# Two mixture-of-experts stages and an S5 scan: a float32 gather, an earlier overflow check, a ring of 18 tiles, S5 products by turns

## The chip, the cores and the metric

The kernel runs on one core of a Trainium2 chip. A core has TensorE (PE, with its weight loads shown as PEld), VectorE (DVE), ScalarE (ACT), GpSimd (POOL) and SyncE (SP, here the queue that issues nearly all DMA). The metric is the device time of one execution in microseconds (us), the median of several runs.

## The reference

256 tokens of width 1024 pass through a first block of two layers (an even mixer, a mixture of experts, an odd mixer, a mixture of experts) and then a second block. The change touches the experts (both layers) and the S5 half of the odd mixer:

```python
def hier_moe(h, ...):                       # 32 experts, 4 groups of 8
    g_top = argmax(hf @ w_group + b_group)  # one group per token
    e_logits = (hf @ w_expert + b_expert)[rows, g_top]
    top_p, top_j = top_k(softmax(e_logits), 2)
    gates = g_w * top_p / sum(top_p)
    # each chosen expert, 1024 -> 512 -> 1024:
    hidden = silu(xb @ w_gate[e]) * (xb @ w_up[e])
    out[token] += (hidden @ w_down[e]) * gate

def s5_mixer(u, ...):                       # 32 groups of 16 channels, 64 complex states each
    bu = einsum('gpc,btgc->btgp', b_bar, u)
    states = associative_scan(x_t = lam_bar * x_{t-1} + bu_t)
    y = einsum('gcp,btgp->btgc', c_mat, states).real + d_skip * u
    z = gelu(y); return z * sigmoid(z @ w_glu)
```

All inputs and outputs are float32. The second block (retention, SSD and a SwiGLU, two layers) is untouched.

## The kernel before

**Stages.** The program is one straight run of instructions for each engine, with four stages in front of the second block: the even mixer, MoE 0, the odd mixer, MoE 1. `moe` handles the experts in eight groups of four; each expert has 32 slots (`SLOTS`), so that a group's four experts fill 128 rows. `expert_group` does, for each group: a *gather* (line 731), products of the token matrix with a one-hot matrix `oh` that picks each slot's token; the gate and up products (line 738), the four experts on TensorE's four column groups of 32, expert after expert in the innermost loop; the down products (line 775); and the scatter back to tokens (lines 785 and 786).

**Weights.** A group needs 24 tiles of 1 MB (8 gate, 8 up, 8 down). `expert_weights` issues them on SP (line 689) into a ring of SBUF tiles: `ring(n, 3, 3)` takes n tiles of the pool `u8` (13 tiles in all) and three each of two other pools. `RINGS = (10, 4)` are the two values of n: the first for MoE 1 and for the first two groups of MoE 0, the second for the later groups of MoE 0, in which pieces of the odd mixer's preparation (`middle`) run as well. A tile's next load waits until TensorE has read it. `AHEAD = 3` rounds of the first group's loads are issued before the stage begins.

**Tokens.** The router's normalised tokens are split for the gather into a high and a low part in TensorE's reduced format (`h_hi`, `h_lo`, 128 x 1024 for each of two token halves): ACT writes the high parts (lines 532 and 535), POOL one low part (line 534), DVE the other in two halves (`low`, line 539). Between them DVE runs the router's chain of small operations (lines 543 to 589), which ends in the slot positions `pos` and in `oh` (line 719). `keep_warm` (line 239) issues products whose results nobody reads.

**Check.** If an expert has more than 32 tokens, `overflowing` computes the rest: every engine loads the largest count (`values_load`, line 663) and branches (`tc.If`, line 664). It stands ahead of group 2, behind five `keep_warm` products. In these data no expert overflows, and the branch jumps over the code.

**S5.** `s5_steps` is a generator; a table (`OPLAN`) says between which steps of the attention its eight parts run. For each n of 8, `turn(n)` makes the input products (line 1675) and DVE and POOL rotate them (lines 1680 to 1683); `scan(n)` runs the recurrence on DVE (line 1693) and rotates back (DVE line 1694, POOL line 1695); `project(n)` multiplies with C (lines 1706, 1711, 1713) into the 32 columns of n. Its 18 products (each float32 product shows as two records) all go to one column group. TensorE's order in the same stretch also holds the projections of the attention, line 317 (`whl` is a weight split by ACT line 293 and DVE line 298).

Of the kernel before, what the change touches and what calls it, by code (L numbers as in the profile page):

```python
# [147 lines left out]
class Model:  # L148
# [369 lines left out]
    def moe(self, l, ahead=None, middle=None, after=None):  # L518
# [114 lines left out]

        n_groups = 32 // GROUP
        for g in range(n_groups):
            last = g == n_groups - 1
            if g == 2:
                self.keep_warm(WARM["check"])
                self.overflowing(l, over["n"], h_hi, h_lo, over["gates"])
# [8 lines left out]
            self.rest = self.expert_group(g, weights, h_hi, h_lo, pos, gate, () if g else (lambda: low(4), gates, beyond), last)  # L648
# [12 lines left out]
    def overflowing(self, l, cint, h_hi, h_lo, gov):  # L661
        nc, tc = self.nc, self.tc
        n = nc.values_load(cint[0:1, 0:1], min_val=0, max_val=T)
        with tc.If(n > SLOTS):
            hT = self.blocks(NK)
            for j0 in range(0, NK, 2):
                pt = self.psum("mm")
                for j in (j0, j0 + 1):
                    for t in range(2):
                        o = (j - j0) * T + t * P  # L670
                        for i, hh in enumerate((h_hi, h_lo)):
                            nc.tensor.matmul(pt[:, o:o + P], hh[t][:, j, :].bitcast(F32), self.ident, start=j == j0 and t == 0 and i == 0,
                                             stop=j > j0 and t == 1 and i == 1, skip_group_check=True)
# [34 lines left out]
    def expert_group(self, g, weights, h_hi, h_lo, pos, gate, meanwhile, last):  # L708
        nc = self.nc
        loads, wg, wu, wd = weights  # L710
        for _ in loads:
            pass
# [9 lines left out]
        for f in meanwhile[:1]:  # L722
            f()
# [1685 lines left out]
```

## Time and profile before

| | |
|---|---|
| median of three runs | 2721.52 us (2717.72 to 2726.39) |
| profiled execution | 2722.02 us, span 2720.2 us |
| TensorE busy | 2421.8 us, 89% of the span |
| VectorE busy | 1261.8 us, 46% |
| granted TensorE clock, mean | 0.957 of full |
| DMA | 660.97 MB, mean 243 GB/s |

How to read it: the profiled execution is one run on the chip; its span is the time from the first to the last recorded instruction, 1.8 us less than the device time. "Busy" shares are means over stages with different limits: the stages lie at about 0 to 186 us (even mixer), to 690 (MoE 0), to 860 (odd mixer), to 1330 (MoE 1), and the second block fills the rest.

### The profile page before, as it was taken

What the parts mean: (1) busy time and instruction counts of PE and PEld (TensorE: products, weight loads), DVE (VectorE), ACT (ScalarE), POOL (GpSimd) and SP (SyncE); (2) the same over time, 40 slices, a digit from 0 to 9 for tenths busy, and PEclk for the clock granted to TensorE, in tenths of its full rate; (3) what the DMA queues carried; (4) which work ended last, traced back from release to release, by engine and by line L of the source; (5) the groups of instructions that cost most, each with busy time, mean ns of one, the idle gap of its engine ahead of it and who ended that gap; (6) DMA issues with size and microseconds to landing.
All of it is one profiled execution on the core that took longest, in us unless ns stands there. A gap on an engine that the chain in (4) does not pass through costs nothing.

```text
span 2720.2 us, 40356 instructions
## 1 busy us (share of the span) xinstructions
PE 2421.8 (89%) x16793; PEld 1811.6 (67%) x16793; DVE 1261.8 (46%) x2071; ACT 950.9 (35%) x1567; POOL 498.9 (18%) x428
## 2 busy tenths in 40 slices
PE   8997777777988778777799998999999999899998
PEld 7862232222776222222489988999988999899997
DVE  5751122201654001000466677565655667855664
ACT  6431100001354000000345565544444455554443
POOL 1120000100321000000223065221113315531110
PEclk9998878899999899989999999999999999999999
DMA  5368999999328999999754533455555353345553
GB/s 184 108 233 356 352 371 411 421 421 407 114 74 315 422 395 421 421 421 421 272 170 140 183 128 109 157 185 173 186 186 170 125 180 130 125 140 185 172 194 139
DMA packets 208793, 660.97 MB, mean 243 GB/s; under 512 B 26554, under 2 KB 33116, under 8 KB 161500
## 3 DMA queue, kind: packets, MB, share of 16 engines
q1 hardware_dynamic: 202148, 657.23, 63.6%
q8 instruction: 135, 2.21, 0.3%
q10 hardware_dynamic: 6456, 1.08, 0.2%
q14 instruction: 54, 0.44, 0.0%
HBM read 657.22 MB, written 1.05 MB: 242 GB/s over the span
## 4 chain that ended last, share of the span: by engine, by line
PE 42%; DMA 13%; DVE 4%; POOL 3%; ACT 2%; issue 1%; SPq 0%; POOLq 0%; ACTq 0%; DVEq 0%
PE ps_mm L317 38%; DMA wx<-in_moe_w_down_dram 5%; DMA wx<-in_moe_w_gate_dram 4%; DMA wx<-in_moe_w_up_dram 4%; DVE whl L298 2%; ACT whl L293 1%; DVE latri L2005 1%; PE ps_sml L2055 1%; PE ps_sml L2019 1%; DVE cv L1871 1%; POOL xn L1956 1%; PE ps_sml L1935 1%; DVE yf L2094 0%; POOL yf L1907 0%; POOL whl L298 0%
## 5 line engine op out<-in xcount | busy, mean ns | idle before, releaser
L317 PE MATMUL ps_mm<-u,whl 128*128 128x256 f32 x8448 | 1056.7, 286 | 25.6 <-POOL whl L298 15.4
L317 PEld LDWEIGHTS ps_mm<-u,whl 128*128 128x128 f32 x8448 | 1035.1, 194 | 37.5 <-POOL whl L298 17.4
L298 DVE TENSOR_TENSOR whl<-w,whl 128x1024 fp32r<-128x1024 f32 x432 | 558.5, 1296 | 437.5 <-ACT whl L293 436.5
L293 ACT ACTIVATE whl<-w 128x1024 fp32r<-128x1024 f32 x472 | 497.3, 1058 | 537.7 <-PE ps_mm L317 509.7
L738 PE MATMUL ps_mm<-wx,xe 128*32 128x512 f32 x2048 | 375.1, 704 | 135.6 <-DMA wx<-in_moe_w_up_dram 92.8
L738 PEld LDWEIGHTS ps_mm<-wx,xe 128*32 128x32 f32 x2048 | 81.4, 125 | 400.5 <-DMA wx<-in_moe_w_up_dram 166.9
L317 PE MATMUL ps_mm<-whl,u 128*128 128x512 f32 x1440 | 343.2, 395 | 3.6 <-ACT u L305 1.8
L317 PEld LDWEIGHTS ps_mm<-whl,u 128*128 128x128 f32 x1440 | 267.3, 189 | 63.6 <-ACT u L305 2.8
L775 PE MATMUL ps_mm<-wx,hid 128*32 128x512 f32 x1024 | 216.0, 613 | 46.2 <-DMA wx<-in_moe_w_down_dram 35.0
L759 DVE TENSOR_TENSOR sl<-sl,ps_mm 128x512 f32<-128x512 f32 x16 | 11.0, 688 | 410.5 <-PE ps_mm L738 301.2
L775 PEld LDWEIGHTS ps_mm<-wx,hid 128*32 128x32 f32 x1024 | 51.4, 110 | 195.9 <-issue 91.1
L383 POOL TENSOR_TENSOR rstd<-rstd,mhalf 128x1 f32<-128x1 f32 x18 | 11.9, 670 | 782.9 <-DVE rstd L382 774.2
L298 POOL TENSOR_TENSOR whl<-w,whl 128x1024 fp32r<-128x1024 f32 x40 | 98.6, 2466 | 237.3 <-ACT whl L293 237.3
L779 DVE SCALAR_TENSOR_TENSOR y_lo<-ps_mm,sg,y_hi 128x512 fp32r<-128x512 f32 x32 | 24.0, 750 | 246.9 <-ACT y_hi L778 245.5
L766 ACT ACTIVATE hid<-ps_sml 128x512 f32<-128x512 f32 x16 | 9.6, 597 | 308.1 <-PE ps_sml L764 308.1
L778 ACT ACTIVATE y_hi<-ps_mm,sg 128x512 fp32r<-128x512 f32 x32 | 22.0, 688 | 232.0 <-PE ps_mm L775 232.0
L731 PE MATMUL ps_sml<-oh,u 128*128 128x128 f32 x512 | 71.7, 305 | 7.7 <-DVE oh L719 4.2
L2200 POOL TENSOR_TENSOR yT<-yT,rb 128x256 f32<-128x256 f32 x44 | 40.9, 950 | 204.1 <-ACT yT L2199 204.1
L731 PEld LDWEIGHTS ps_sml<-oh,u 128*128 128x128 f32 x512 | 69.5, 221 | 11.7 <-DVE oh L719 4.6
L758 ACT ACTIVATE sl<-ps_mm 128x512 f32<-128x512 f32 x16 | 9.6, 597 | 187.9 <-PE ps_mm L738 174.6
L305 ACT ACTIVATE u<-yf 128x256 fp32r<-128x256 f32 x124 | 48.5, 413 | 71.0 <-DVE yf L2094 19.2
L1871 DVE SCALAR_TENSOR_TENSOR cv<-ps_mm,cols_cw,cv 128x253 f32<-128x253 f32 (+1 forms) x144 | 64.1, 476 | 19.4 <-ACT cv L1868 18.5
(522 smaller groups left out, 2251.9 us busy)
## 6 DMA issues: line engine op xcount, KB each, us to landing
wx<-in_moe_w_gate_dram SPq DMA_DIRECT2D x128, 1024.0 KB
wx<-in_moe_w_up_dram SPq DMA_DIRECT2D x128, 1024.0 KB
wx<-in_moe_w_down_dram SPq DMA_DIRECT2D x128, 1024.0 KB
w<-in_w_in_dram SPq DMA_DIRECT2D x104, 1024.0 KB
w<-in_w_gate_up_dram SPq DMA_DIRECT2D x44, 1024.0 KB
w<-in_w_down_dram SPq DMA_DIRECT2D x20, 1024.0 KB
w<-in_ret_out_dram SPq DMA_DIRECT2D x16, 1024.0 KB
w<-in_ssd_out_dram SPq DMA_DIRECT2D x16, 1024.0 KB
```

The costliest lines, as they stand in the source:

```text
L293: ins = nc.scalar.activation(hi, src, AF.Copy)
L298: eng.tensor_tensor(lo, src, hi.bitcast(F32), op=OP.subtract)
L305: self.nc.scalar.activation(hi, src, AF.Copy)
L317: ins = nc.tensor.matmul(out, a, b, start=start and i == 0, stop=stop and i == 2)
L731: nc.tensor.matmul(pg[:, o:o + P], hh[t][:, j, :], oh2[:, t, :], start=j == j0 and i == 0, stop=j == j0 + 3 and i == 3)
L738: nc.tensor.matmul(out[r, :], xe[:, k, r], w[k // 4][a][:, k % 4, :], start=k == 0, stop=k == NK - 1, tile_position=(0, a * SLOTS))
L775: nc.tensor.matmul(py[r, :], hid[:, m, r], wd(c, m, a), start=m == 0, stop=m == 3, tile_position=(0, a * SLOTS))
L1871: V.scalar_tensor_tensor(acc[:, s:], ps[:, :T - s], cw[i][:, b + m:b + m + 1], acc[:, s:], op0=OP.mult, op1=OP.add)
L1935: ins = E.matmul(py[:, o:o + T], v[0, h // 2][:, c0:c0 + P], sc[:, :T], start=b == b0, stop=False, skip_group_check=True)
L1956: G.tensor_tensor(f, hi, lo, op=OP.add)
L2005: eng.tensor_tensor(x_, tri.unsqueeze(1).to_broadcast([P, 4, P]), lar[part][:, c, h0:h0 + 4].bitcast(F32).unsqueeze(2).to_broadcast([P, 4, ...
L2200: nc.gpsimd.tensor_tensor(sil[s0][:, m, :], sil[s0][:, m, :], sc[1], op=OP.mult)
```

## The change

The tokens are kept in float32, in one `u8` tile `h` written by two ACT instructions; the splits on POOL and DVE are gone, and a group's gather has 16 float32 products in place of 32 in the reduced format. `gates`, `beyond` (the largest count) and the check run in group 0: the first two ahead of the gather, the check right behind it and ahead of the gate products. The loads of group 0 that don't fit ahead are issued behind the check. The `keep_warm` in front of the check is gone. The rings get 12 and 5 tiles of `u8`, and a fourth round of the first loads is issued ahead of the router's chain. In S5, `turn` takes two n and alternates their products, `project` takes four n and alternates between the four column groups, and the rotated inputs lie in tiles of another pool.

```diff
-RINGS = (10, 4)
+RINGS = (12, 5)
...
-        h_hi = [self.u4([P, NK, P], "hi", F32R) for _ in range(2)]
-        h_lo = [self.u4([P, NK, P], "lo", F32R) for _ in range(2)]
-        tc.keep_in_program_order(A.activation(h_hi[0], xg[0], AF.Copy, scale=rr[0]))
-        A.activation(xg[0], xg[0], AF.Copy, scale=rr[0])
-        G.tensor_tensor(h_lo[0], xg[0], h_hi[0].bitcast(F32), op=OP.subtract)
-        A.activation(h_hi[1], xg[1], AF.Copy, scale=rr[1])
-
-        def low(j0):
-            js = slice(j0, j0 + 4)
-            tc.keep_in_program_order(V.scalar_tensor_tensor(h_lo[1][:, js], xg[1][:, js], rr[1], h_hi[1][:, js].bitcast(F32), op0=OP.mult, op1=OP.subtract))
+        h = self.u8([P, 2, NK, P])
+        for t in range(2):
+            tc.keep_in_program_order(A.activation(h[:, t], xg[t], AF.Copy, scale=rr[t]))
+        next(weights[0])
...
+        def check():
+            self.overflowing(l, over["n"], h, over["gates"])
+
...
-            if g == 2:
-                self.keep_warm(WARM["check"])
-                self.overflowing(l, over["n"], h_hi, h_lo, over["gates"])
...
-            self.rest = self.expert_group(g, weights, h_hi, h_lo, pos, gate, () if g else (lambda: low(4), gates, beyond), last)
+            self.rest = self.expert_group(g, weights, h, pos, gate, () if g else (gates, beyond, check), last)
...
-        for _ in loads:
+        for _ in () if meanwhile else loads:
             pass
...
-        for f in meanwhile[:1]:
+        for f in meanwhile[:2]:
             f()
...
-                for i, (t, hh) in enumerate(((0, h_hi), (0, h_lo), (1, h_hi), (1, h_lo))):
-                    nc.tensor.matmul(pg[:, o:o + P], hh[t][:, j, :], oh2[:, t, :],
-                                     start=j == j0 and i == 0, stop=j == j0 + 3 and i == 3)
+                for t in range(2):
+                    nc.tensor.matmul(pg[:, o:o + P], h[:, t, j, :], oh2[:, t, :], start=j == j0 and t == 0, stop=j == j0 + 3 and t == 1)
             nc.scalar.activation(xe[:, j0:j0 + 4, :], pg.rearrange("p (a s) -> p a s", a=4), AF.Copy)
+
+        for f in meanwhile[2:]:
+            f()
+        for _ in loads:
+            pass
...
-        for f in meanwhile[1:]:
-            f()
...
-        def project(n):
+        def project(bp):
+
+            ps = self.psum("mm")
+            parts = [live.pop(4 * bp + i)[:2] for i in range(4)]
...
+                for j, (k, w, c) in enumerate(((0, 0, 0), (1, 1, 1), (2, 1, 0), (2, 0, 1))):
+                    for i, part in enumerate(parts):
+                        rows = slice(32 * i, 32 * i + 32)
+                        E.matmul(ps[rows, b * T + P:(b + 1) * T], cc["CT"][k][:, bb, rows], part[w][:, b, c], start=False, stop=False,
+                                 skip_group_check=True, tile_position=(0, 32 * i))
...
-        for n in range(10):
-            if n < 8:
-                turn(n)
-            if 0 <= n - 1 < 8:
-                scan(n - 1)
-            if n >= 2:
-                project(n - 2)
-            yield
+        turn(0, 1)
+        yield
+        scan(0)
+        yield
+        turn(2, 3)
+        scan(1)
+        yield
+        scan(2)
+        yield
+        turn(4, 5)
+        scan(3)
+        yield
+        scan(4)
+        project(0)
+        yield
+        turn(6, 7)
+        scan(5)
+        yield
+        scan(6)
+        yield
+        scan(7)
+        yield
+        project(1)
+        yield
```

What the change moves is seen in the engines' order of instructions. The first place is TensorE at the start of MoE 0, from the router's last products (`mk`) through the gather to the first gate products (`wx` is a weight tile, `xe` the gathered tokens). Before:

```order
L585 MATMUL ps_sml_2032<-mk_2029,c_masks 128x64
L586 MATMUL ps_sml_2032<-mk_2029,c_ones 128x32
L239 MATMUL ps_sml_2035<-c_masks 128x384
L731 MATMUL ps_sml_2085<-oh_2080,u_289_1991 128x128
L731 MATMUL ps_sml_2085<-oh_2080,u_290_1992 128x128
...
L731 MATMUL ps_sml_2103<-oh_2080,u_289_1991 128x128
L731 MATMUL ps_sml_2103<-oh_2080,u_290_1992 128x128
L738 MATMUL ps_mm_2121<-wx_1736,xe_2084 32x512
L738 MATMUL ps_mm_2121<-wx_1738,xe_2084 32x512
```

And now (line numbers are a little lower in the changed file: 723 is the gather, 734 the gate):

```order
L578 MATMUL ps_sml_2036<-mk_2034,c_masks 128x64
L579 MATMUL ps_sml_2036<-mk_2034,c_ones 128x32
L239 MATMUL ps_sml_2039<-c_masks 128x384
L618 MATMUL ps_sml_2076<-mk_2034,c_ones 128x32 x2
L723 MATMUL ps_sml_2087<-oh_2060,u_289_1991 128x128
L723 MATMUL ps_sml_2097<-oh_2060,u_289_1991 128x128
L723 MATMUL ps_sml_2087<-oh_2060,u_289_1991 128x128 x7
L723 MATMUL ps_sml_2097<-oh_2060,u_289_1991 128x128 x7
L656 TENSOR_LOAD cint_2081
L657 COMPARE_AND_BRANCH
...
L657 UNCONDITIONAL_BRANCH
L734 MATMUL ps_mm_2325<-wx_1736,xe_2086 32x512
L734 MATMUL ps_mm_2325<-wx_1738,xe_2086 32x512
```

The products of line 618 that count tokens (line 625 before, behind the gate products) stand ahead of the gather, and the load of the count and the branch stand between the gather and the gate. The second place is SP at the same point, where the loads of group 0's last tiles now are behind the branch:

```order
L681 DMA wx_2309<-in_moe_w_down_dram 128x2048
L681 DMA wx_2311<-in_moe_w_down_dram 128x2048
L656 TENSOR_LOAD cint_2081
L657 COMPARE_AND_BRANCH
...
L657 UNCONDITIONAL_BRANCH
L681 DMA wx_2313<-in_moe_w_down_dram 128x2048
L681 DMA wx_2315<-in_moe_w_down_dram 128x2048
```

Of the down tiles of group 0, six are behind the branch, and none were before. The third place is TensorE in S5. Before, `project(0)` follows the products of `turn(2)` and ends in line 317:

```order
L1675 MATMUL ps_sml_4825<-u_843_4563,u_520_3110 128x128
L1706 MATMUL ps_mm_4846<-u_843_4563,s5cb 32x128
L1711 MATMUL ps_mm_4846<-s_ad_4765,u_508_3074 32x128
L1713 MATMUL ps_mm_4846<-s_ad_4765,u_508_3074 32x127
L1711 MATMUL ps_mm_4846<-s_ad_4765,u_508_3074 32x128
L1713 MATMUL ps_mm_4846<-s_ad_4765,u_509_3075 32x127
...
L1713 MATMUL ps_mm_4846<-s_ad_4765,u_509_3075 32x127
L317 MATMUL ps_mm_4775<-whl_4772,u_847_4567 128x512 x6
```

And now, with the beginning of `project(0)` and of `project(1)` (lines 1701, 1708 and 1712; `u_874`, `u_883`, `u_903` and `u_935` each hold the rotated states of two n):

```order
L317 MATMUL ps_mm_4827<-whl_4728,u_845_4412 128x512 x6
L1701 MATMUL ps_mm_4862<-u_842_4409,s5cb 32x128 x4
L1708 MATMUL ps_mm_4862<-u_874_4620,u_507_3000 32x128 x2
L1708 MATMUL ps_mm_4862<-u_883_4688,u_507_3000 32x128
L1508 MATMUL ps_sml_4964<-c_ident,qa_4752 128x128 x4
...
L1568 MATMUL ps_sml_5166<-c_odd,c_ident 128x128
L1701 MATMUL ps_mm_5183<-u_842_4409,s5cb 32x128 x4
L1708 MATMUL ps_mm_5183<-u_903_4805,u_507_3000 32x128 x2
L1708 MATMUL ps_mm_5183<-u_935_5055,u_507_3000 32x128 x2
L1712 MATMUL ps_mm_5183<-u_903_4805,u_507_3000 32x127 x2
L1712 MATMUL ps_mm_5183<-u_935_5055,u_507_3000 32x127 x2
```

Eight blocks of 18 products became two of 72, in which the column group changes with each product; the first is interleaved with transposes (line 1508) and `turn(6, 7)`, and the second stands behind all of the attention's projections.

## Rows read from the trace of the kernel before

**Rows 1.** page, shares of the chain by engine

```profile
PE 42%; DMA 13%; DVE 4%; POOL 3%; ACT 2%; issue 1%; SPq 0%; POOLq 0%; ACTq 0%; DVEq 0%
```

**Rows 2.** windows of MoE 0: us, five engines busy, PEclk, DMA share, GB/s

```profile
280.00:290.00 10.00, 8.39 (x40) 2.31 (x39) 0.00 (x0) 0.60 (x1) 0.00 (x0) 1.00 1.02 424
290.00:300.00 10.00, 8.56 (x32) 2.31 (x33) 1.17 (x2) 1.72 (x3) 0.00 (x0) 1.00 0.84 329
300.00:310.00 10.00, 7.10 (x37) 4.87 (x35) 6.13 (x32) 3.57 (x9) 0.00 (x0) 0.91 0.79 303
390.00:400.00 10.00, 10.00 (x77) 4.01 (x76) 0.00 (x0) 0.75 (x2) 0.00 (x0) 0.82 0.31 103
```

**Rows 3.** windows of MoE 1 around its check

```profile
955.00:960.00 5.00, 4.59 (x23) 1.47 (x24) 1.00 (x2) 1.37 (x2) 0.00 (x0) 1.00 0.84 306
960.00:965.00 5.00, 4.64 (x16) 2.56 (x14) 2.88 (x5) 0.00 (x0) 0.00 (x0) 1.00 0.58 205
965.00:970.00 5.00, 4.95 (x36) 4.05 (x37) 0.17 (x1) 1.19 (x2) 0.00 (x0) 1.00 0.97 390
```

**Rows 4.** page, DMA issues with KB each

```profile
wx<-in_moe_w_gate_dram SPq DMA_DIRECT2D x128, 1024.0 KB
```

**Rows 5.** timeline of router 0, DVE and POOL: start, us, instructions

```profile
190.62 0.28 DVE L568 TENSOR_TENSOR cmp<-es 128x128 f32<-128x128 f32 x1
190.64 2.47 POOL L534 TENSOR_TENSOR u<-xg,u 128x1024 fp32r<-128x1024 f32 x1 [2.36 <-ACT xg L533]
190.82 2.43 DVE L569 TENSOR_TENSOR cmp<-ceq,c_places 128x128 f32<-128x128 f32 x1
```

**Rows 6.** timeline of PE, router 0 to group 0's gate

```profile
195.62 7.04 PE L731 MATMUL ps_sml<-oh,u 128*128 128x128 f32 x32
202.59 8.69 PE L738 MATMUL ps_mm<-wx,xe 128*32 128x512 f32 x64
211.21 0.63 PE L625 MATMUL ps_sml<-mk,c_ones 128*128 128x32 f32 x4
```

**Rows 7.** timeline of PE at MoE 0's check

```profile
301.01 3.47 PE L239 MATMUL ps_sml<-c_masks 128*128 128x384 f32 x10
305.27 0.24 PE L259 MATMUL ps_mm<-c_ident,vrows 60*128 60x60 f32 x1 [0.79 <-PEq L664]
...
311.30 1.12 PE L731 MATMUL ps_sml<-oh,u 128*128 128x128 f32 x4 [3.41 <-issue]
```

**Rows 8.** waits of SP's queue, 180 to 215 us: total, times, longest

```profile
SPq L689 <- PE ps_mm L738: 23.8, 2, 22.4
```

**Rows 9.** timeline of PE, S5 blocks

```profile
709.78 0.40 PE L1706 MATMUL ps_mm<-u,s5cb 32*32 32x128 f32 x2
...
713.77 0.38 PE L1711 MATMUL ps_mm<-s_ad,u 128*32 128x128 f32 x2
713.99 0.38 PE L1713 MATMUL ps_mm<-s_ad,u 128*32 128x127 f32 x2
714.30 3.02 PE L317 MATMUL ps_mm<-whl,u 128*128 128x512 f32 x12
...
796.42 0.38 PE L1713 MATMUL ps_mm<-s_ad,u 128*32 128x127 f32 x2
```

**Rows 10.** line 1426: ns min/median/max, first and last start

```profile
L1426 PE MATMUL ps_sml<-u,s_z x64: 241/241/263, 383.6 to 384.5; 128*32 128x32 f32 x64
```

**Rows 11.** windows of the odd stage, and of line 1426

```profile
696.00:782.00 86.00, 78.95 (x502) 63.70 (x502) 61.87 (x99) 28.89 (x86) 38.22 (x32) 0.96 0.24 83
696.00:796.80 100.80, 93.75 (x602) 75.84 (x601) 66.14 (x104) 35.39 (x95) 38.22 (x32) 0.97 0.24 82
380.00:390.00 10.00, 8.27 (x97) 7.74 (x97) 4.09 (x9) 0.60 (x1) 0.69 (x3) 0.50 1.00 416
```

**Rows 12.** timelines of POOL and DVE at the end of the last scan

```profile
779.00 1.73 POOL L1695 TENSOR_TENSOR s_ad<-s_zz,u 128x512 f32<-128x512 f32 x1 [1.98 <-DVE s_zz L1693]
783.06 1.23 DVE L298 TENSOR_TENSOR whl<-w,whl 128x1024 fp32r<-128x1024 f32 x1 [3.48 <-ACT whl L293]
```

More of the change, by code (lines that the diff above doesn't have):

```diff
@@ L24 @@
 GROUP = 4
-WARM = dict(start=4, router=6, places=1, check=5)
+WARM = dict(start=4, router=6, places=1)
 U8 = 13
-RINGS = (10, 4)
+RINGS = (12, 5)
 AHEAD = 3
@@ L664, in overflowing @@
         with tc.If(n > SLOTS):
-            hT = self.blocks(NK)
+            halves = [self.s("ov_x", [P, 4, T]) for _ in range(2)]
+            hT = [halves[j // 4][:, j % 4] for j in range(NK)]
             for j0 in range(0, NK, 2):
@@ L670, in overflowing @@
                         o = (j - j0) * T + t * P
[L671 to L673 removed]
+                        nc.tensor.transpose(pt[:, o:o + P], h[:, t, j, :], self.ident)
                 for j in (j0, j0 + 1):
@@ L706, in expert_weights, with expert_group @@
         return loads(), wg, wu, down
-    def expert_group(self, g, weights, h_hi, h_lo, pos, gate, meanwhile, last):
+    def expert_group(self, g, weights, h, pos, gate, meanwhile, last):
         nc = self.nc
         loads, wg, wu, wd = weights
-        for _ in loads:
+        for _ in () if meanwhile else loads:
             pass
@@ L1662, in s5_steps, with turn @@
         keep = self.tc.keep_in_program_order
-        py = [None] * 4
         live = {}
-        def turn(n):
-            bp, i = divmod(n, 4)
-            rows = slice(32 * i, 32 * i + 32)
-            cs, sn = (cc["tabs"][2 * bp + i // 2][:, j, :, i % 2].unsqueeze(2).to_broadcast([P, 2, 2, P]) for j in range(2))
-            pb = self.psum("sml")
+        def turn(*ns):
+            pbs = [self.psum("sml") for _ in ns]
             for b in range(2):
                 for c in range(2):
-                    o = pb[:, (b * 2 + c) * P:(b * 2 + c + 1) * P]
@@ L1682, in turn @@
-            G.tensor_tensor(a[:, :, 0], a[:, :, 0], d[:, :, 1], op=OP.add)
-            G.tensor_tensor(a[:, :, 1], a[:, :, 1], d[:, :, 0], op=OP.subtract)
-            live[n] = a, d, cs, sn
+                        for n, pb in zip(ns, pbs):
+                            bp, i = divmod(n, 4)
+                            rows = slice(32 * i, 32 * i + 32)
+                            E.matmul(pb[:, (b * 2 + c) * P:(b * 2 + c + 1) * P], cc["BT"][l][rows, 2 * bp + b, c, :],
+                                     uT[rows, 2 * bp + b, 1 - l], start=b == 0 and c == 0 and l == 0,
+                                     stop=b == 1 and c == 1 and l == 1, skip_group_check=True)
@@ new lines, in turn @@
+            for n, pb in zip(ns, pbs):
+                bp, i = divmod(n, 4)
+                cs, sn = (cc["tabs"][2 * bp + i // 2][:, j, :, i % 2].unsqueeze(2).to_broadcast([P, 2, 2, P]) for j in range(2))
+                p4 = pb.rearrange("p (b c t) -> p b c t", b=2, c=2)
+                ad = self.u4([P, 2, 2, 2, P], "ad")
+                a, d = ad[:, 0], ad[:, 1]
+                V.tensor_tensor(a, p4, cs, op=OP.mult)
+                V.tensor_tensor(d, p4, sn, op=OP.mult)
+                G.tensor_tensor(a[:, :, 0], a[:, :, 0], d[:, :, 1], op=OP.add)
+                G.tensor_tensor(a[:, :, 1], a[:, :, 1], d[:, :, 0], op=OP.subtract)
+                live[n] = a, d, cs, sn
```

63 lines of the change are left out of this document (25 added, 38 removed).

## The prediction

> **What bounds the kernel now.** I read the shares of the chain first, then windows stage by stage, then the rows where a stage's limit shows. The chain is TensorE's for 42% and DMA's for 13% [rows 1]; the second block, which the change leaves as it is, is most of TensorE's part. Two limits matter for the change.
>
> In both MoE stages DMA is the limit: its share stands at 1.01 or 1.02, at 424 GB/s [rows 2]. A weight tile of 1024 KB [rows 4] then takes 1,048,576 / 424,000 = 2.47 us, and whatever leaves the queue idle moves the end by as much. It is idle mainly at three places. Ahead of group 0 SP waits 22.4 us for a gate product, since the ring is full [rows 8]: what ends late there is the router, the gather and the first reads. Around the check the share falls to 0.84 and 0.79 in MoE 0 and to 0.84, 0.58 and 0.97 in MoE 1 [rows 2, 3]. At 390 us it falls to 0.31 [rows 2], where the short ring of MoE 0 is waited for.
>
> In the odd mixer TensorE is the limit. From 696 us to 796.8 us (the end of the last `project`) it is busy 93.75 of 100.8 us [rows 11], with DVE at 66.14. The recurrences end much earlier than `project(7)`: POOL's last rotation is 779.00 + 1.73 = 780.7 us [rows 12], and TensorE needs 16 us more, the last of it for `project(7)` [rows 9].
>
> **S5, the largest term.** One `project(n)` takes 714.30 - 709.78 = 4.52 us [rows 9], and eight take 36.2 us: 36 records each, of which a pair starts every 0.22 us (713.77 to 713.99), about 108 ns a record. The four column groups by turns are shown by line 1426: 64 records start within 383.6 to 384.5 us, 14 ns apart, each 241 ns long [rows 10], while the clock was at 0.50 of full, 1.2 GHz [rows 11]. They have 32 columns. A record of 128 columns that takes 108 ns alone would take 108 x 32 / 128 x 2 = 54 ns there without overlap; 14 ns is a quarter. So I take 108 / 4 = 27 ns a record: 144 records are 3.9 us, two blocks 7.8 us, and TensorE loses 28.4 us of work. From below it is 14 ns a record (4 us for both blocks), from above no overlap (31 us for both). `turn` by pairs of row groups saves up to half of its roughly 16 us; no row shows row groups of 32 by turns, so I count nothing and keep 0 to -8.
>
> With 93.75 - 28.4 = 65 us of work in this stretch TensorE is no longer last; DVE is. It did 61.87 us from 696 to 782 us [rows 11], which takes in all recurrences; the new order puts two more weight splits ahead of the last recurrence (1.23 us each, [rows 12]), 64.3 us. At the share at which it ran then, 61.87 / 86 = 0.72, it ends at 785.3 us; at 0.95 at 763.7 us. Freed of TensorE's pace it should come between: 0.81, 775.4 us. Behind it come POOL's 1.73 us and `project(1)` with 3.9 us, which nothing hides any more: 781.0 us, against 796.8. **Term: -16 us**, with -6 and -27 as ends. TensorE, in order, now stalls for `scan(3)` ahead of `project(0)`, with later projections and `turn(6, 7)` queued behind, and for `scan(7)` ahead of `project(1)`; these waits are inside the DVE reckoning. What follows in the stage, and MoE 1's first loads, move along.
>
> **The gather itself: nothing.** 16 float32 products are 32 records, as 32 of the reduced format were. One pair of the latter took 7.04 / 16 = 0.44 us at the lower clock [rows 6]; a float32 pair of 128 columns takes 0.22 us at full clock [rows 9], twice as fast at twice the clock. The work hidden here is under DMA in groups 1 to 7 anyway.
>
> **The router's chain: -2.1 us in each MoE.** DVE line 569 took 2.43 us where line 568, of the same shape, took 0.28, and POOL line 534 ran 2.47 us over just that time [rows 5]. I read this as DVE held by POOL; with line 534 gone, 2.15 us go, in MoE 1, whose code is the same, as well. If line 569 is slow by itself, nothing. From this stage 0.63 us are given back in MoE 0, where the counting products now stand ahead of the gather (line 625, [rows 6]). Net -1.5 and -2.1.
>
> **The check's old place: -3.9 and -3.2 us.** In MoE 0 the loss was 10 x (1.01 - 0.84) + 10 x (1.01 - 0.79) = 3.9 us [rows 2], in MoE 1 5 x (0.17 + 0.43 + 0.04) = 3.2 us [rows 3]. These go; the ring is not late at group 2 for any other reason that shows.
>
> **The check's new place: +2.1 and +3.2 us.** TensorE's branch took from 301.01 to 305.27, 4.26 us, of which `keep_warm` hid 3.47 [rows 7]. Now nothing stands there but the end of the gather, and behind it wait the gate products, whose reads free the ring. If about ten records are queued when the sequencer reaches the branch, as those of `keep_warm` may have been, they hide 10 x 0.22 = 2.2 us at the lower clock (7.04 / 32, [rows 6]), and 10 x 0.108 = 1.1 us at the full one: 2.1 and 3.2 us remain. From below 0.8 each (as covered before); from above 4.26, plus 3.41 us of "issue" idle that followed the jump in MoE 0 [rows 7]. SP's branch stands in the same shadow: its six down tiles can't start before gate tiles are read. DVE and ACT have only the evacuation of the gather, which doesn't wait for the branch.
>
> The Trainium skill, "Runtime: NRT & Kernel Launch", section Instruction fetch mechanics, speaks against the new place: a taken branch whose target is outside the prefetched window must fetch it before execution goes on. The 3.41 us behind the first jump agree with it, the second jump showed none. By that rule at both places the terms would be 7.7 us each and the sum 10 us higher, and this is a rival below; by the rows it is 2.1 and 3.2.
>
> **The rings.** In the kernel before, a free tile of `u8` served as an eleventh, so the ring held 17 and now 18: one tile more is loaded in the idle time ahead of group 0, -2.5 us in each MoE. For the rest of MoE 0 the ring has 11 in place of 10; of the 7.0 us lost at 390 us [rows 2] it may save one tile's time or most of it: -3 us, with 0 and -7 as ends. The fourth round of loads and the other pool for S5's tiles cost nothing: SP waits for the ring there anyway [rows 8].
>
> **The sum.** MoE 0: -3.9 - 2.5 - 3 - 1.5 + 2.1 = -8.8. MoE 1: -3.2 - 2.5 - 2.1 + 3.2 = -4.6. Odd mixer -16. Second block 0 (its order is the same but for its first rows). Together -29.4 from the profiled execution's 2722.0 us, 0.5 above the median: **2692.6 us**.
>
> **Rivals.**
> *The column groups don't overlap at 128 columns.* For it: the record's spacing of 108 ns might be a weight load's time and not the columns'. Against it: line 1426, whose records load weights too. TensorE stays the limit of the stage, 0 us there: 2722 - 13.4 = 2708.6.
> *The branch costs its whole length plus the refetch.* 7.7 us in both places in place of 2.1 and 3.2: +10, 2702.7. The rows on the first jump speak for it; against it, MoE 1 showed no such idle behind its check (TensorE busy 4.95 of 5 us, [rows 3]).
> *Slower.* TensorE's in-order waits for `scan(3)` and `scan(7)` hold back line 317 and so the attention, whose operations DVE then waits for, a ring of waits in the odd stage. Its price is DVE's share: the stage ends later than before when 696 + 64.3 / share + 5.6 exceeds 796.8, at a share under 0.68, and the gain of 13.4 us in the MoE stages is lost too under 0.59. At 0.5 the stage ends at 830.2: 2742. Against it: `project(1)` no longer shares TensorE with 16 us of trailing work.
>
> **Chances.** Forecast (DVE at 0.72 to 0.95, branch partly hidden) 0.64; no overlap 0.09; the branch whole 0.15; slower 0.05; the rest, several terms a few us off on the bad side, 0.07. About 0.3%, 8 us, is what a measurement tells from no change. Faster by more (under 2713.4) takes the first and third nearly whole, and most of the second: 0.87; the same 0.08; slower 0.05. The low end, 2673, has the stage at -27, the ring at -7 and the branch covered as before (-11 - 4 - 3.7); the high end, 2711, takes in no overlap and 2 us more. The forecast's own range is 2678 (the stage alone at -27, and the branch covered) to 2703 (the stage at -6).
>
> **What would show it.** Lines 1708 and 1712: starts about 27 ns a record apart, a block under 5 us. Odd stage: TensorE idle ahead of both blocks, DVE's share above 0.72, `project(1)` ending near 780 less what MoE 0 gained. Line 563 (569 before) under 0.4 us. No dip of DMA's share in group 2; the branch instead between gather and gate, TensorE idle for 2 to 3 us. It would be wrong if the two blocks took 15 us each, or if TensorE idled over 7 us behind the new branch.

## The result and the profile after

| | before | after |
|---|---|---|
| median, same chip | 2719.62 us (4 runs, 2715.05 to 2726.39) | 2683.06 us (4 runs, 2681.3 to 2684.27) |
| profiled execution | 2722.02 us | 2682.83 us, span 2680.7 us |

The ratio is 0.986 (95%: 0.9842 to 0.9878): 36.6 us faster by medians, 39.2 us between the two profiled executions. The forecast of 2692.6 us had the sign and the range right and was 9.5 us too slow. Five points of the timelines, found in both kernels, divide the 39.2 us:

| stretch (profiled executions, us) | before | after | change | forecast |
|---|---|---|---|---|
| start to router 0's logits (DVE `lg`) | 188.42 | 190.88 | +2.5 | 0 |
| MoE 0, to the copy of S5's input on DVE | 508.98 | 491.27 | -17.7 | -8.8 |
| odd mixer, to the last `project` record's end | 99.40 | 81.88 | -17.5 | -16 |
| rest of the odd mixer, to router 1's logits | 62.62 | 60.98 | -1.6 | 0 |
| MoE 1, to its last scatter product's start | 472.74 | 464.65 | -8.1 | -4.6 |
| second block | 1389.86 | 1393.17 | +3.3 | 0 |

The second block's code is the same in all kernels of this study. In their profiled executions it took 1385.4 to 1389.9 us in the kernel before and its two versions with S5's part, and 1387.0 to 1393.7 in the eleven kernels built on the changed one. So the +3.3 us may belong to the change; no run tells.

The page of the changed kernel, the chain by engine (TensorE's share as before, DMA's 16% in place of 13%):

```profile
PE 42%; DMA 16%; DVE 5%; POOL 3%; ACT 2%; SPq 1%; issue 1%; POOLq 0%; ACTq 0%; DVEq 0%
```

Windows of the changed kernel (columns as in [rows 2]): group 2 of MoE 0, where the check stood (its gather now starts at 295.7 us); the place of the late ring (the gather that stood at 384.7 us before starts at 375.0), two windows; group 2 of MoE 1 (its gather starts at 925.5 us); the odd mixer up to its last `project`; and the same up to the end of DVE's last rotation:

```profile
290.00:300.00 10.00, 9.96 (x64) 5.88 (x63) 3.89 (x6) 2.43 (x4) 0.00 (x0) 1.00 1.02 425
380.00:390.00 10.00, 10.00 (x94) 3.36 (x94) 5.14 (x34) 0.96 (x2) 0.47 (x2) 1.00 1.02 424
390.00:400.00 10.00, 6.32 (x34) 1.21 (x30) 0.00 (x0) 0.00 (x0) 0.00 (x0) 0.87 1.01 420
925.00:930.00 5.00, 5.00 (x39) 4.03 (x38) 2.27 (x4) 1.19 (x2) 0.00 (x0) 1.00 1.01 413
682.00:764.00 82.00, 62.25 (x592) 49.48 (x590) 68.10 (x105) 36.35 (x98) 38.11 (x32) 0.85 0.27 94
682.15:759.10 76.95, 57.76 (x460) 45.85 (x458) 65.50 (x101) 32.99 (x90) 36.96 (x32) 0.84 0.29 100
```

DMA's share, 0.84, 0.31 and 0.58 in [rows 2, 3], is 1.01 or 1.02. In the odd mixer TensorE went from 93.75 of 100.8 us [rows 11] to 62.25 of 82, and DVE, at 0.83, is now the busier. The timeline of TensorE in the changed kernel, first router 0 to group 0's gate (line 723 is the gather, 734 the gate), then the same in MoE 1, then S5:

```profile
190.60 4.12 PE L239 MATMUL ps_sml<-c_masks 128*128 128x384 f32 x12
...
196.10 3.82 PE L723 MATMUL ps_sml<-oh,u 128*128 128x128 f32 x32
200.74 7.44 PE L734 MATMUL ps_mm<-wx,xe 128*32 128x512 f32 x64 [0.82 <-ACTq L657]
...
832.09 0.71 PE L723 MATMUL ps_sml<-oh,u 128*128 128x128 f32 x4 [1.70 <-ACT u L532]
833.13 3.39 PE L723 MATMUL ps_sml<-oh,u 128*128 128x128 f32 x28 [0.33 <-ACT u L532]
837.54 7.07 PE L734 MATMUL ps_mm<-wx,xe 128*32 128x512 f32 x64 [1.02 <-ACTq L657]
...
717.29 1.12 PE L1508 MATMUL ps_sml<-c_ident,qa 128*128 128x128 f32 x4 [4.92 <-POOL qa L1498]
...
722.27 0.42 PE L1708 MATMUL ps_mm<-u,u 128*32 128x128 f32 x1 [1.44 <-DVE u L1690]
...
751.97 1.11 PE L1508 MATMUL ps_sml<-c_ident,qa 128*128 128x128 f32 x4 [4.77 <-POOL qa L1498]
757.96 0.42 PE L1701 MATMUL ps_mm<-u,s5cb 32*32 32x128 f32 x8
...
759.18 0.30 PE L1708 MATMUL ps_mm<-u,u 128*32 128x128 f32 x1 [0.45 <-DVE u L1690]
...
760.31 0.30 PE L1708 MATMUL ps_mm<-u,u 128*32 128x128 f32 x1 [0.48 <-POOL u L1691]
...
762.08 0.43 PE L1708 MATMUL ps_mm<-u,u 128*32 128x128 f32 x8
762.32 0.40 PE L1712 MATMUL ps_mm<-u,u 128*32 128x127 f32 x8
...
763.19 0.40 PE L1712 MATMUL ps_mm<-u,u 128*32 128x127 f32 x8
```

The gate now waits 0.82 and 1.02 us at the branch, and by the rows both waits end with ACT's branch, not with TensorE's own (`<-ACTq L657`; the profile infers who ends a wait). The branch on TensorE's queue (PEldq) and on ACT's, with min/median/max in ns and the first and last start in us, and ACT's evacuation of the gather's second half in MoE 0:

```profile
L657 PEldq COMPARE_BRANCH  x2: 367/1352/2337, 199.3 to 834.8; - x2
L657 ACTq COMPARE_BRANCH  x2: 45/45/45, 200.5 to 837.1; - x2
```

```profile
199.96 0.60 ACT L724 ACTIVATE xe<-ps_sml 128x512 f32<-128x512 f32 x1 [0.97 <-PE ps_sml L723]
```

In MoE 0 TensorE's branch took 0.37 us from 199.3 us on and was over before the gather ended at 199.92. ACT, in its own order, comes to the check only behind that evacuation's start; its branch stands at 200.5 us, and the gate starts at 200.74. In MoE 1 TensorE's branch took 2.34 us, to 837.1, and ACT's stands at 837.1 too.

In MoE 1 the gather waits for the tokens (`u`, line 532): ACT, in its own order, wrote them behind the router's two exponentials. In S5 eight records begin every 0.22 us, (763.19 - 762.32) / 32 = 27 ns each; in [rows 9] two did. The waits for the recurrences are 1.44, 0.45 and 0.48 us; the long ones are for POOL's line 1498 of the attention, at four places 1.55 + 4.92 + 3.19 + 4.77 = 14.4 us. In the kernel before two waits of that kind show, 5.8 us in all; the trailing products of TensorE covered the others.

DVE at router 0 of the changed kernel (562 and 563 were 568 and 569):

```profile
193.08 0.28 DVE L562 TENSOR_TENSOR cmp<-es 128x128 f32<-128x128 f32 x1
193.28 0.28 DVE L563 TENSOR_TENSOR cmp<-ceq,c_places 128x128 f32<-128x128 f32 x1
```

Line 563 takes 0.28 us in place of 2.43 [rows 5].

### The profile page after: what moved, and what is told of

Same layout as the page of the kernel before. It is cut to its first block, busy times and chain, and to the rows that moved or that the text cites. A ratio compares the mean times of both kernels' runs of the same rounds, so it can differ in the third digit from the quotient of the medians.

```text
span 2680.7 us, 40349 instructions
## 1 busy us (share of the span) xinstructions
PE 2371.3 (88%) x16773; PEld 1773.3 (66%) x16773; DVE 1260.7 (47%) x2067; ACT 949.0 (35%) x1565; POOL 492.3 (18%) x426
## 4 chain that ended last, share of the span: by engine, by line
PE 42%; DMA 16%; DVE 5%; POOL 3%; ACT 2%; SPq 1%; issue 1%; POOLq 0%; ACTq 0%; DVEq 0%
PE ps_mm L317 38%; DMA wx<-in_moe_w_down_dram 6%; DMA wx<-in_moe_w_up_dram 5%; DMA wx<-in_moe_w_gate_dram 4%; DVE whl L298 2%; ACT whl L293 1%; DVE cv L1885 1%; DVE latri L2019 1%; PE ps_sml L2069 1%; PE ps_sml L2033 1%; DMA w<-in_w_in_dram 1%; DVE yf L2108 1%; SPq L681 1%; PE ps_sml L1949 1%; POOL xn L1970 0%
## 5 line engine op out<-in xcount | busy, mean ns | idle before, releaser
L734 PE MATMUL ps_mm<-wx,xe 128*32 128x512 f32 x2048 | 369.6, 683 | 140.5 <-DMA wx<-in_moe_w_up_dram 93.7
L306 DVE TENSOR_TENSOR u<-yf,u 128x256 fp32r<-128x256 f32 x124 | 60.2, 514 | 9.4 <-ACT u L305 9.4
L723 PE MATMUL ps_sml<-oh,u 128*128 128x128 f32 x512 | 62.1, 280 | 2.0 <-ACT u L532 2.0
```

What stands on the lines that cost most here:

```text
L306: self.nc.vector.tensor_tensor(lo, src, hi.bitcast(F32), op=OP.subtract)
L723: nc.tensor.matmul(pg[:, o:o + P], h[:, t, j, :], oh2[:, t, :], start=j == j0 and t == 0, stop=j == j0 + 3 and t == 1)
L734: nc.tensor.matmul(out[r, :], xe[:, k, r], w[k // 4][a][:, k % 4, :], start=k == 0, stop=k == NK - 1, tile_position=(0, a * SLOTS))
```

## The experiments

Each starts from the changed kernel ("after", 2683.06 us) unless it says otherwise. "MoE 0", "MoE 1" and "odd mixer" are the stretches of the table above, against after's 491.27, 464.65 and 81.88 us. Ratios are to the kernel before on the same chip.

The runs were made on several chips, on which the medians of the kernel before were 2719.4 to 2723.4 us, so a difference of 2 or 3 us between the medians of two runs shows little by itself. The stages, each from one profiled execution, say more. In the two runs that change S5 alone MoE 0 took 490.4 and 491.2 us. MoE 1 took 464.6 us in the run with the shorter later ring, and 466.1 and 466.3 in the two runs on S5, whose first gather there took 6.06 us in place of 4.43.

**S5 as before.**

```diff
-        turn(0, 1)
-        yield
-        scan(0)
...
+        for n in range(10):
+            if n < 8:
+                turn(n)
...
```

> The changed kernel (2682.8 us in its profiled execution) with S5 as before: one turn per n, one project per n, eight blocks on one column group each. Theory: the turned products give the odd stage its gain. From the evacuation of the S5 inputs (682.15 us) to the end of the last project (763.95) the changed kernel takes 81.8 us and the kernel before took 99.4; the stage should go back to about 99, TensorE busy over 90% of it, and the time to 2700 (2697 to 2703). Rival: the stage is shorter because weights come earlier with the larger ring, and S5's order gives little: the stage stays under 87 us and the time under 2688.

Measured: 2702.2 us, ratio 0.9935 (0.9909 to 0.9961); 19.1 us slower than after. Odd mixer 101.4 us, 19.5 more than in after. So S5's part is the largest term, as forecast.

**The blocks of 72 products, but column group after column group.**

```diff
-            for b in range(2):
-                bb = 2 * bp + b
-                for i in range(4):
-                    rows = slice(32 * i, 32 * i + 32)
...
+            for i, part in enumerate(parts):
+                rows = slice(32 * i, 32 * i + 32)
+                for b in range(2):
+                    bb = 2 * bp + b
...
```

> The changed kernel with the two S5 blocks of 72 products kept where they are, but with the column group in the outermost loop, so that 18 products in a row go to one group. Theory (overlap of the column groups): records 108 ns apart in place of 27, each block 15.6 us in place of 3.9; the second block has nothing beside it, so at least +11.7 us, and +23 if the first isn't hidden either: 2695 to 2706. Rival (the gain is in making two late blocks out of eight, and not in the turns): records still overlap or the blocks lie where TensorE is idle anyway, 2682 to 2687.

Measured: 2696.9 us, 0.9913 (0.9884 to 0.9942); 13.8 us slower than after. Its timeline of TensorE in the second block, and its window of the stage:

```profile
775.89 0.38 PE L1706 MATMUL ps_mm<-u,u 128*32 128x128 f32 x2
776.11 0.38 PE L1708 MATMUL ps_mm<-u,u 128*32 128x127 f32 x2
776.33 0.38 PE L1706 MATMUL ps_mm<-u,u 128*32 128x128 f32 x2
```

```profile
682.60:777.30 94.70, 85.42 (x593) 68.86 (x593) 68.67 (x106) 36.93 (x98) 37.56 (x32) 0.93 0.25 81
```

The same products start 108 ns apart again, and TensorE is busy 85.42 of 94.7 us, DVE for as long as in after. The odd mixer took 94.3 us. So the overlap of column groups, the disputed step, is worth 12.5 of the 19.5 us in the stage (13.8 of 19.1 by medians); by difference, the rest goes to the new order and `turn` by pairs, which no run separates.

**The check at group 2 again, behind five `keep_warm` products.**

```diff
+            if g == 2:
+                self.keep_warm(5)
+                check()
...
-(gates, beyond, check)
+(gates, beyond)
```

> The changed kernel with the check back ahead of group 2, behind five unread products. Theory: at the old place it costs DMA 3.9 us in MoE 0 and 3.2 us in MoE 1, and at the new place nearly nothing, since the sequencer takes the branch while the gather still runs; the gate's wait there of 0.82 and 1.02 us is mostly the gather's evacuation (0.60 us) and falls by 0.2 to 0.4 only. So +6 us: 2689 (2686 to 2692), with DMA shares near 0.8 at group 2 of both MoE stages. Rival (a longer ring rides over the check at group 2): no dip there, and 2682 to 2684.

Measured: 2688.33 us, 0.9883 (0.9857 to 0.9908); 5.3 us slower than after; MoE 0 +3.0, MoE 1 +2.7 us. Its windows at group 2 of either stage:

```profile
290.00:295.00 5.00, 4.96 (x16) 2.50 (x15) 3.77 (x6) 2.66 (x3) 0.00 (x0) 1.00 0.49 203
295.00:300.00 5.00, 3.97 (x24) 2.82 (x23) 0.78 (x5) 0.22 (x1) 0.00 (x0) 1.00 0.77 261
...
925.00:930.00 5.00, 4.69 (x16) 2.66 (x15) 2.94 (x5) 0.00 (x0) 0.00 (x0) 1.00 0.43 125
```

DMA loses 5 x (0.52 + 0.24) = 3.8 us and 5 x 0.58 = 2.9 us here, and nothing in after. Against the run without a check, below, the old place costs 3.4 us in MoE 0 and 2.8 in MoE 1.

**No check at all.**

```diff
-(gates, beyond, check)
+(gates, beyond)
```

> The changed kernel without the check for overflow: neither the load of the count nor the branch runs, and tokens beyond an expert's 32 slots would be left out (there are none in these data). It prices the check at its new place. By the theory (most of the branch lies under the gather and its evacuation) TensorE's wait ahead of the first gate products, 0.82 us in MoE 0 and 1.02 us in MoE 1 behind the check, stays near 0.8 us for the evacuation in MoE 0, and the loads behind the check begin a few us sooner without use, since they wait for gate tiles anyway: 0 to 2 us faster than the changed kernel, 2681 to 2683. By the prediction's terms (+2.1 and +3.2) it would be 5 us faster: 2678. By the rival that the branch costs 7.7 us at each place it would be 15 us faster: 2668.

Measured: 2681.88 us (2677.16 to 2682.66), 0.9842 (0.9816 to 0.9868); MoE 0 -0.5, MoE 1 -0.1 us. In its timeline the gate begins when the gather ends, with no wait:

```profile
195.87 3.82 PE L723 MATMUL ps_sml<-oh,u 128*128 128x128 f32 x32
199.62 4.93 PE L734 MATMUL ps_mm<-wx,xe 128*32 128x512 f32 x44
```

So the 0.82 and 1.02 us come with the check; without it the gate starts before ACT evacuates the gather's second half (199.72 us). By the stages the check now costs 0.5 + 0.1 us, not the 5.3 of the forecast; the 1.2 us between the medians is less than this run's spread of 5.5 us.

**POOL's operation of line 534's size again**, on tiles that nobody waits for.

```diff
+        G.tensor_tensor(xg[0], xg[0], h[:, 0], op=OP.subtract)
         next(weights[0])
```

> The changed kernel with one POOL subtraction of 128 x 1024 put back behind the first token half, as line 534 was; nobody reads what it writes. Theory: DVE's comparison (0.28 us in the changed kernel) takes 2.4 us again, as it is held by POOL; TensorE waits 2 us for the mask, the granted clock falls to half and the first gather of MoE 0 takes 7 us in place of 3.8. So about +2.1 and +3.2 us in MoE 0, and little in MoE 1, where the tokens come later from ACT than the mask from DVE: 2688 (2685 to 2691). Rival (the comparison was slow by its own operands, and the clock fell for another reason): it stays at 0.28 us, and the time at 2683.

Measured: 2686.66 us, 0.9878 (0.985 to 0.9907); +3.6; MoE 0 +1.3, MoE 1 +3.0 us. Its timelines of POOL and of DVE in MoE 0, and of TensorE's gather in MoE 1:

```profile
190.92 2.35 POOL L533 TENSOR_TENSOR xg<-xg,u 128x1024 f32<-128x1024 f32 x1
```

```profile
191.50 0.16 DVE L542 TENSOR_REDUCE tp_m<-lg 128x2 f32<-128x8 f32 x1
191.70 1.73 DVE L545 SCALAR_TENSOR_TENSOR tp_c<-lg,tp_m,c_places 128x4 f32<-128x4 f32 x2
...
194.83 0.28 DVE L564 TENSOR_TENSOR cmp<-ceq,c_places 128x128 f32<-128x128 f32 x1
```

```profile
838.19 5.02 PE L724 MATMUL ps_sml<-oh,u 128*128 128x128 f32 x28 [0.33 <-ACT u L532]
```

Other instructions are held, a pair of 4 elements that takes 0.36 us in after, until POOL ends (191.70 + 1.73 = 193.43; POOL 193.27), and line 564 is quick. Line 569 was not slow by itself. The hold of 1.4 us fits the +1.3 of MoE 0. The +3.0 of MoE 1, where the expectation had little, is another matter: POOL's operation starts there at 837.18 us, behind the router's chain, but the warming products took 5.65 in place of 4.12 us and this part of the gather 5.02 in place of 3.39, at a granted clock of 0.72 (828 to 834 us) and 0.55 (838 to 841 us) in place of 1.00. So the run shows nothing of the router's term in MoE 1. In MoE 0 the gather still ran at full clock (3.82 us), but TensorE idled 1.19 us ahead of the mask, not the 1.97 of the kernel before, so whether POOL's work had a part in the clock there stays open.

**The later groups' ring of MoE 0 shorter by one tile.**

```diff
-RINGS = (12, 5)
+RINGS = (12, 4)
```

> The changed kernel (2683 us) with the later groups of MoE 0 on a ring of 4 + 6 tiles as before, in place of 5 + 6. Theory: the dip of DMA's share to 0.31 at 390 us, which cost 7 us, went because of the eleventh tile; with ten it comes back, +5 us (3 to 7): 2688. Rival: it went because the odd mixer's preparation now runs in other groups or at a higher clock, and the ring gives nothing: no dip, 2682 to 2684.

Measured: 2685.41 us, 0.9862 (0.9841 to 0.9883); +2.4; MoE 0 +2.9, MoE 1 -0.1 us. Its windows at 370 to 390 us, where after stands at 1.01 and 1.02:

```profile
370.00:380.00 10.00, 9.94 (x128) 7.80 (x132) 2.46 (x5) 1.19 (x2) 0.17 (x2) 0.75 0.89 369
380.00:390.00 10.00, 8.57 (x72) 2.63 (x68) 5.14 (x34) 0.60 (x1) 0.46 (x2) 1.00 0.77 299
```

The loss is 1.2 + 2.4 = 3.6 us, half of the 7.0 us at this place before. In this stage the ring is worth its -3, though by ratio the run can't be told from after (0.9862 and 0.986); something else took the other half.

**One tile less in the long ring**, its memory held by a tile that isn't used.

```diff
-RINGS = (12, 5)
+RINGS = (11, 5)
...
+        held = self.held = self.u8([P, 2, NK, P])
...
```

> The changed kernel with one u8 tile held back through each MoE stage, so that 17 tiles are loaded ahead of the check in place of 18, as before the change. Theory: the time ahead of group 0 is idle for DMA, so the tile costs 2.5 us in each stage: +5 us, 2688 (2686 to 2690); more if a ring of 17 also runs dry later. Rival: the idle ahead of group 0 is ended by the router's chain in any case and the ring's length is made up later: within 1.5 us, 2682 to 2685.

Measured: 2686.13 us, 0.9863 (0.9843 to 0.9884); +3.1; MoE 0 +3.4, MoE 1 +2.7 us: a tile's 2.47 us in each stage, and a little more. By ratio this run can't be told from after either.

**Three warming products in place of six** behind the router.

```diff
-WARM = dict(start=4, router=6, places=1)
+WARM = dict(start=4, router=3, places=1)
```

> The changed kernel with three unread products behind the router in place of six, so that TensorE stands idle for about 2 us ahead of the mask in both stages, as it did before the change (1.97 us). Theory: that idle time is what brought the clock to 0.50 in the first gather of MoE 0 before; the gather takes 7 us in place of 3.8 and the gate products begin 3 us later: +3 to +4 us, 2686 to 2687. Rival: the clock fell for another reason (it stayed at 1.00 with 1.19 us of idle time there): gather at 3.8 us, 2682 to 2684.

Measured: 2684.35 us (2678.77 to 2691.97), 0.9856 (0.9829 to 0.9882): unclear by the medians. In its profiled execution MoE 0 took 2.8 and MoE 1 7.9 us longer. Its timeline of TensorE, the gather of MoE 0, then MoE 1:

```profile
196.16 5.11 PE L723 MATMUL ps_sml<-oh,u 128*128 128x128 f32 x32
...
834.82 6.67 PE L723 MATMUL ps_sml<-oh,u 128*128 128x128 f32 x32 [1.69 <-ACT u L532]
845.25 3.64 PE L734 MATMUL ps_mm<-wx,xe 128*32 128x512 f32 x16 [3.77 <-PEq L657]
```

In MoE 1 the gather took 6.67 us in place of 4.1, and the wait at the branch was 3.77 us in place of 1.02; here TensorE's own branch ended it (`<-PEq L657`). In MoE 0 the gather took 5.11 us in place of 3.82. TensorE had stood idle ahead of the mask for 1.75 and 1.74 us. So in this execution idle time and a low clock went together, as the theory has it; the run with S5's part alone, below, had 1.97 us of idle time and the full clock.

**Tokens ahead of the exponentials on ACT, the gather's first half kept first.**

```diff
-        A.activation(ge, ge, AF.Exp)
+        tc.keep_in_program_order(A.activation(ge, ge, AF.Exp))
...
+                    if meanwhile and j == 4 and t == 0:
+                        self.tc.keep_in_program_order(ins)
```

> The changed kernel with two places of its order mended: in MoE 1 ACT writes the tokens ahead of the two small exponentials (it did so behind them, and TensorE waited 1.70 and 0.33 us), and in group 0 of both stages the gather fills its first half before its second, so that the first evacuation (0.60 us) runs beside the second half. Theory: gate products of group 0 begin 0.6 to 0.8 us earlier in MoE 0 and about 2.6 us earlier in MoE 1, and DMA with them: 2680 (2678.5 to 2681). Rival: the branch, of 2.3 us on TensorE's weight queue in MoE 1, takes the place of these waits: 2682 to 2684.

Measured: 2680.28 us (5 runs), 0.9843 (0.9826 to 0.986). In MoE 1 the gather's waits are gone and the gate starts 10.28 us behind the logits in place of 12.53, but the stage takes 464.4 us, as in after. An earlier start of the gate gains nothing any more there; later ones do cost: behind the logits the gate was 1.4 us later than in after with S5 as before, 2.9 with POOL's operation and 5.0 with three warming products, and MoE 1 took 1.5, 3.0 and 7.9 us longer.

**The same with a ring of 11 and 5.**

```diff
-RINGS = (12, 5)
+RINGS = (11, 5)
```

> The run with early tokens and gather halves (2680.3 us), and the first ring written with 11 u8 tiles in place of 12. The pool still has a twelfth free, so 18 tiles are loaded ahead as with 12; but the input tile of the even mixer's last projection goes back to a slot that is free earlier. With 12 it took the slot that the last normalisation still reads, ACT's first of two copies waited 1.1 us for it, and the router began at 190.2 us in place of 188.4. Theory: the router begins at 188.5 to 189.2 us and all of MoE 0 moves along: 2679 (2677.5 to 2680). Rival: the router is late because of the clock (0.50 at 170 to 175 us) or of DMA's load there, and not because of the slot: no change, 2680 to 2681.

Measured: 2679.04 us (5 runs), 0.984 (0.982 to 0.986), the fastest of all, though its lead of 1.2 us on the run above is inside both spreads. The instruction that had waited for the twelfth tile's memory at the end of the even mixer no longer did (TensorE's line 317 there began at 168.79 in place of 170.17 us), but its products then ran at a granted clock of 0.50, and router 0's logits were at 189.91 us, 1 us earlier than in after: memory and clock aren't told apart.

**The kernel before with S5's part alone.**

```diff
-        for n in range(10):
-            if n < 8:
-                turn(n)
...
+        turn(0, 1)
+        yield
+        scan(0)
...
```

> The kernel before, with S5's part of the change alone. Theory: the odd stage's gain belongs to S5 alone and adds to that of the MoE stages: taking S5 out of the changed kernel cost 19 us, so putting it in gains about as much, 2701 against 2720 (-16 to -21 us), from the S5 inputs' evacuation to the end of the last project 80 to 84 us in place of 99.4. Rival: the stage needs the changed kernel's earlier weights or its pool of tiles to get below 90 us: a gain under 10 us.

Measured: 2708.19 us (6 runs, 2698.41 to 2714.09), 0.9949 (0.993 to 0.9968). Odd mixer 81.8 us, as in after; but the median gains 12.1 us where the stage gained 17.6. The profiled execution was the fastest of the six, here and in the next run.

**The same with nine warming products in place of six** behind the router.

```diff
-WARM = dict(start=4, router=6, places=1, check=5)
+WARM = dict(start=4, router=9, places=1, check=5)
```

> The kernel before with the S5 part of the change, and nine in place of six warming products behind the router, which fill the 1.97 us in which TensorE idles ahead of the router's mask products. The S5 part alone gave 12.1 us by medians where its stage gave 17.6 us, with a wide spread. If the spread comes from the granted clock at the gathers (3.90 us in one execution and 7.04 in another for the same code), the median is 3 to 8 us lower than with the S5 part alone, 2700 to 2705, the gather takes 3.8 us in both MoE stages, and the spread is under 6 us. If the clock there has nothing to do with it, the median stays at 2706 to 2710 and the spread at 10 us or more.

Measured: 2702.73 us (6 runs, 2691.65 to 2709.95), 0.9929 (0.9904 to 0.9953). The median is 5.5 us lower, as the theory of the clock has it, but the spread is as wide as before and the intervals overlap. But the gathers of group 0, where the theory had it, took 3.90 us in both. MoE 0 took 5.9 us less, and the difference stands at a later gather of the stage, at 380 us. First the timeline and the window of S5's part alone, then those with nine products:

```profile
381.85 7.09 PE L731 MATMUL ps_sml<-oh,u 128*128 128x128 f32 x32
```

```profile
385.00:390.00 5.00, 5.00 (x27) 4.15 (x30) 0.00 (x0) 1.19 (x2) 0.00 (x0) 0.50 0.50 206
390.00:395.00 5.00, 5.00 (x32) 1.15 (x28) 0.00 (x0) 0.00 (x0) 0.00 (x0) 0.61 0.01 3
```

```profile
380.13 3.95 PE L731 MATMUL ps_sml<-oh,u 128*128 128x128 f32 x32
```

```profile
385.00:390.00 5.00, 5.00 (x52) 1.45 (x48) 0.00 (x0) 0.00 (x0) 0.00 (x0) 1.00 0.58 192
390.00:395.00 5.00, 3.71 (x24) 1.11 (x16) 3.05 (x17) 0.60 (x1) 0.19 (x1) 1.00 0.99 418
```

Same code here, same ring of 10 and 4 tiles, TensorE idle for the same 7.13 us ahead of the products in front of the gather: at a granted clock of 0.50 of full, 1.2 GHz, the gather took 7.09 us and DMA lost 8.6 us from 380 to 400; at 1.00, 2.4 GHz, it took 3.95 and lost 2.1.

## Why the prediction was right, and where its terms were off

**S5 (-16; measured -17.5): right, by its own steps.** 27 ns a record, so the rival without overlap is out; DVE is the busiest engine, and `project(1)` is exposed at the end. Up to the end of its last rotation DVE was busy 65.50 of 76.95 us, a share of 0.85, where the forecast had 64.3 us at 0.81. That 0.81 was chosen between 0.72 and 0.95, and no row spoke for it: that the size came out so near is in part luck. The last rotation ends 77 us behind the copy of S5's input (forecast 775.4 - 697.4 = 78), and `project(1)` 4.9 us later (forecast 5.6); the block itself took 6.1 us from its first product, 757.96 us, with its waits, not under 5. That DVE sets the pace is read from its share; no run changes DVE's work. The saving of `turn` by pairs, counted as 0 to -8, is there in TensorE's busy time, 16.9 us before and 9.8 after:

```profile
L1675 PE MATMUL ps_sml<-u,u 32*128 32x128 f32 x128 | 16.9, 278 | 0.0
```

```profile
L1667 PE MATMUL ps_sml<-u,u 32*128 32x128 f32 x128 | 9.8, 299 | 0.0
```

By the shares it matters little, since TensorE is no longer the busiest. That DVE isn't at 0.95 is in part the attention's: DVE waits 5.2 us in all for POOL (line 274), and POOL for DVE ahead of line 1498, which I had not priced; in-order waits for the recurrences, the rival "slower", came to 2.4 us.

**The check's old place (-3.9 and -3.2): right.** The dips are gone, and cost 3.0 and 2.7 us when put back (3.4 and 2.8 against no check).

**The check's new place (+2.1 and +3.2): the step that was mis-sized.** 0.82 and 1.02 us of wait, worth 0.5 and 0.1 us in the stages. The forecast reckoned with TensorE's branch behind ten records. In MoE 0 that branch took 0.37 us and was hidden whole, and the wait is for ACT's branch, which the forecast put at nothing: the evacuation doesn't wait for the branch, as it says, but the gate waits for ACT to come to the branch. The rival of 7.7 us each is out in after. TensorE's own branch took 0.37 us in MoE 0 and 2.34 in MoE 1, and waits that it ended were 1.24 and 1.31 us (the two runs with tokens ahead of the exponentials) and 3.77 us (three warming products), all in MoE 1. The Trainium skill, "Runtime: NRT & Kernel Launch", section Instruction fetch mechanics, says that a taken branch whose target isn't in the prefetched window must fetch it before execution goes on. A fetch may be part of these waits, but no run here shows it, nor why one and the same branch differs so.

**Tile and rings (-2.5 each, -3): right in size,** 3.4, 2.7 and 2.9 us by the runs that take them back. But of the 7.0 us lost at 390 us the ring explains the half only: with the old ring of 10 and 4, the run with nine warming products lost 2.1 us there, its gather at full clock, and the one with six lost 8.6, its gather at half. So the rest went with TensorE's granted clock in that gather; I had read all of it as the ring's.

**Router (-1.5 in MoE 0, -2.1 in MoE 1): right in mechanism.** Line 563 takes 0.28 us, and the run with POOL's operation shows the hold on other instructions in MoE 0. In MoE 1 of the kernel before line 569 took 2.44 us as well, as the forecast had it. In MoE 0 the gate starts 14.17 - 9.86 = 4.3 us sooner after the logits: 2.15 of it here, and 7.04 - 3.82 = 3.2 in the gather, the clock again (1.00 in place of 0.56 and 0.50 from 195 to 205 us), less the branch and the counting. I had put the gather down as nothing "at the lower clock"; that it might run at the higher one I did not price. In MoE 1 the gain was eaten by the tokens' late place on ACT: the gate starts 12.53 us after the logits, 11.52 before.

**Where the missing 9 us of MoE 0 come from.** By the runs: check 3.0, tile 3.4, ring 2.9; by the traces: gate sooner 4.3, the clock's part at 390 us 7.0 - 2.9 = 4.1. These give 17.7; the last two are worked out and not tested singly, and that the sum meets the measured 17.7 proves none of its parts. The clock at these two gathers, 3.2 + 4.1 = 7.3 us, is most of what the forecast missed. It set out from one execution of the kernel before in which both ran at about half clock and didn't price that they might not; with S5's part alone the first ran at full clock from the same instructions, and with nine warming products both did. So no run shows that these 7.3 us belong to the change and not to that execution. In MoE 1 check and tile give 5.4 of 8.1 us; 2.7 us I can't assign. Router 0's logits are 2.5 us later: 1.1 us of it is a longer wait that the run with a ring of 11 and 5 doesn't have, but its logits came only 1 us earlier. With S5's part alone, whose code and rings are those of the kernel before up to there, they came at 190.21 us, so most of the 2.5 us isn't shown to be the change's.

**Open.** Why the kernel before (2711.08 to 2728.51 us in eleven runs on one chip) and its two versions with S5's part spread over 16 to 18 us, and after and most runs on it over 3 to 9. The clock at the gather at 380 us is one cause in the two executions with a trace; the others have none.

## What to carry to other kernels

Small products that use 32 columns of TensorE should change the column group with each product; check then what becomes the limit, since here DVE became the busiest engine when the stage was 17.5 us shorter, while TensorE's work in it fell by some 30 us. A branch belongs where engines are late anyway, not where a full ring waits for them; and every engine's way to it counts, since here TensorE waited for ACT there. Before a dip in DMA is put down to a short ring, read the granted clock of the products that free its tiles.

## What the runs showed of the hardware

- Float32 records of 128 columns in four column groups by turns start 27 ns apart at full clock, though each lasts 0.27 to 0.29 us; in one group they start 108 ns apart.
- A DVE instruction of 0.28 us took 2.43, and a pair of 0.36 us took 1.73, beside a POOL operation of 2.4 us, until POOL was done, while a reduction just ahead of it, with one input, took its 0.16 us. The Trainium skill, "SBUF — State Buffer", section Who interferes with whom, has an exclusive lock there: a DVE instruction with two SBUF inputs waits for a POOL instruction that reads SBUF. Both rows agree.
- The granted clock at one place differs between executions and kernels with the same instructions there: group 0's gather of the kernel before took 7.04 us in one execution, at a granted clock of 0.50 to 0.56, and 3.90 us with S5's part, at 1.00, behind the same wait of 1.97 us for the router; why stays open.
